# A decoder block on one core: SBUF pools moved by 32 and 96 bytes

## The chip, the core and the metric

The kernel runs on one NeuronCore of a Trainium2 chip. The metric is device time in microseconds for one execution of the whole program. TensorE multiplies, and loads its stationary operand (the weights, `lhsT`) with an instruction of its own that overlaps the matmul before it; the moving operand is the right-hand one (`rhs`). VectorE (DVE), ScalarE (ACT) and GpSimd (POOL) do elementwise work, and SyncE (SP) and ScalarE issue DMAs. All operands of TensorE lie in SBUF, whose 128 partitions each hold a row of bytes; "address" below always means the byte offset within that row, the same in all partitions.

## The reference

One residual block with 2048 positions and a width of 1024, in float32:

```python
mod = silu(c) @ w_mod + b_mod;  shift, scale, gate = split(mod, 3)
h = rms_norm(x, g_norm) * (1 + scale) + shift
x_rnn, z_rnn, q, k, v, z_attn, g_r, g_a = split(h @ w_in, 8)      # each 1024 wide
xc = causal_depthwise_conv(x_rnn)                                   # width 4
y_rnn = (rg_lru(xc) * silu(z_rnn)) @ w_out_rnn                      # gated scan, 8 blocks of 128
o = dilated_attention_mixture(rope(q), rope(k), v)                  # 8 heads of 128, 3 windows
y_attn = (o * silu(z_attn)) @ w_out_attn
merged = sigmoid(g_r + b) * y_rnn + sigmoid(g_a + b) * y_attn
out = rms_norm(x + gate * (merged @ w_o), g_final)
```

## The kernel before, in words

**How a float32 product is made.** Each float32 operand is split into a high part, rounded to the type `float32r`, and a low part that holds the rest. `mm3` (L151 to L154 of the kernel) then makes a product from three matmuls: high by high, high by low, low by high. Every call ends in `mm`, so nearly all matmuls of the profile carry line L149. In a pair of names such as `X<-T,S` the first name is the PSUM tile, and the two behind the arrow are the operands.

**The stages.** The input projection comes first, in two halves `f` of 1024 positions.

- At the start of each half the values `v` are made directly (`values`): the stationary operand is a piece of the normalized activations (tiles `T`, or `b12h` and `b12l`), the moving one is a weight tile `S`, 256 columns wide. A call makes 96 matmuls; there are 16 calls' worth.
- All other columns go through `strassen`, which makes a 2x2 block product with seven multiplications instead of eight. Here the stationary operand is a weight block `S` (seven slots, `S0` to `S6`) and the moving one is an activation block `T` (fourteen slots), 512 columns wide. One multiplication, `prod`, is 12 matmuls in a row: four steps of `mm3`. There are 28 pairs of column blocks, two halves and seven products, so 28 x 2 x 7 x 12 = 4704 matmuls. Between products the rest of the recurrent branch slips in a few: its gates (`xh`, `xl` by `gh`, `gl`), and transposes.
- Then attention, 16 head-halves. It mixes scores (`kq`, `q1`), transposes (`pp` with the identity `cs`) and sums (`pth`, `ptl` by `vh` or `wh`) with the two branch projections, which are fed in a few steps at a time (`steps`): moving `yh` and `yl`, stationary `S`, 512 columns. Two branches, four column blocks each, eight row blocks and 24 matmuls give 1536.
- The end is the output projection (`output`), four quarters of four row blocks, two column halves and eight steps of `mm3`: 768 matmuls, moving `oh` and `ol`, stationary `mh` and `ml`, 512 columns. It alternates with what is left of `steps`, and finishes alone.

**What sets the order.** Inside the input projection and attention the program writes the order out by hand (`manual_schedule`); steps hang on the number of products done (`run_late`, `pump`). Weight blocks are made in the first half (load of `R`, high part on ScalarE at L157, low part on GpSimd at L163, store to DRAM) and loaded again in the second, seven slots ahead (`load_next`). SyncE issues loads and most stores, ScalarE the stores of weight blocks.

**Where tiles lie.** SBUF is filled from both ends. Pools opened on the left stack upward: `cp` (constants), then `hp` with the fourteen slots of `T`, then the working pools of the stage; in attention `ap` and at the end `fp` take the place of `hp`. Pools opened with `side="right"` stack downward: `pS` (`S0` to `S3`), `pR`, `wS` (`S4` to `S6`), `wq`, and later `fl` (`yh`, `yl`). Every tile is rounded up to 32 bytes. The lines that open the pools around the change are L482 to L492:

```python
    B = {}
    hp = pools.open("hp", bufs=1)
    ...
    pS = pools.open("pS", side="right", bufs=1)
    pR = pools.open("pR", side="right", bufs=1)
    wS = pools.open("wS", side="right", bufs=1)
```

The built program gives these first addresses; all other slots of a name follow at multiples of 1024 bytes or more, and the pieces of a tile that one matmul reads start at multiples of 512 bytes in it, so each name has one remainder on division by 256 (only the keys of the window scores start at any multiple of 128 bytes in `kq`):

| operand | role | first address before | modulo 256 | after | modulo 256 |
|---|---|---|---|---|---|
| `T` | moving in `strassen`, stationary in `values` | 18528 | 96 | 18560 | 128 |
| `S0` | stationary in `strassen` and `steps`, moving in `values` | 212960 | 224 | 212864 | 128 |
| `b12h`, first half | stationary in `values` | 149248 | 0 | 149280 | 32 |
| `b12h`, second half | stationary in `values` | 141536 | 224 | 141568 | 0 |
| `yh` | moving in `steps` | 159712 | 224 | 159616 | 128 |
| `oh` | moving in `output` | 18528 | 96 | 18560 | 128 |
| `mh` | stationary in `output` | 108640 | 96 | 108672 | 128 |
| `kq` | both, in scores | 22112 | 96 | 22144 | 128 |
| `pth` | moving in sums | 125856 | 160 | 125888 | 192 |
| `vh` | stationary in sums | 105376 | 160 | 105408 | 192 |
| `xh` | moving in gates | 170144 | 160 | 170176 | 192 |
| `gh` | stationary in gates | 168096 | 160 | 168128 | 192 |

Of the kernel before, what the change touches and what calls it, by code (L numbers as in the profile page):

```python
# [10 lines left out]
F32 = mybir.dt.float32  # L11
# [9 lines left out]
P = 128  # L21
# [68 lines left out]
def decoder_block(ctx, tc, x, c, positions, g_norm, w_mod, b_mod, w_in, b_gate, conv_w, conv_b,  # L90
# [4 lines left out]
    def T(pool, shape, dt, tag, **kw):  # L95
        cnt[0] += 1
        return pool.tile(shape, dt, tag=tag, name=f"{tag}_{cnt[0]}", **kw)
# [25 lines left out]
    cp = ctx.enter_context(tc.tile_pool(name="cp", bufs=1))  # L123
# [32 lines left out]
    def hi_act(o, i):  # L156
        nc.scalar.activation(o, i, AF.Copy)  # L157
# [190 lines left out]
    def strassen(up, f, key, done):  # L348
# [7 lines left out]
        def take():  # L356
            if f:
                return (f, *loaded.pop(0))
            i = next(n_op)
            return f, i, first.pop(i)  # L360

        def prod(ps, b, first, last, op=None):
            f, i, s = op or take()
            bh, bl = B[b]
            for k in range(KH):
# [114 lines left out]


    B = {}  # L482
    hp = pools.open("hp", bufs=1)

    def slot():
        return T(hp, [P, KH, CH], F32R, "T", bufs=14)


    pS = pools.open("pS", side="right", bufs=1)
    pR = pools.open("pR", side="right", bufs=1)  # L490
    wS = pools.open("wS", side="right", bufs=1)
# [35 lines left out]
    def build(st, names, xs, k, first=False, keep=None, pt=None):  # L527

        hh, hl = B[names[k // KH]]
        if pt is None:  # L530
# [13 lines left out]
    def operand(name):  # L544
        B[name] = (slot(), slot())

# [4 lines left out]
    def build_odd(st, xs):  # L551

        B["B12"] = (T(st, [P, KH, CH], F32R, "b12h"), T(st, [P, KH, CH], F32R, "b12l"))
        operand("B22")
        f32 = lambda b, i, k: B[b][i][:, k, :].bitcast(F32)
        tt = nc.vector.tensor_tensor
# [8 lines left out]
        def split(name, k, t):  # L565
            hh, hl = B[name]
            hi_act(hh[:, k, :], t)
            lo_dve(hl[:, k, :], t, hh[:, k, :])
# [1326 lines left out]
```

## Time and profile before

| | |
|---|---|
| median of three runs | 2258.73 us |
| lowest, highest | 2254.85, 2258.97 us |
| span of the profiled execution | 2256.2 us |
| the profiled execution's own time | not given beside its span; the span lies between the lowest and the highest run |
| TensorE busy | 2212.2 us, 98% of the span, 11422 matmuls |
| weight loads busy | 1856.8 us, 82% |
| VectorE, ScalarE, GpSimd busy | 1346.9 (60%), 1257.3 (56%), 977.8 us (43%) |
| mean granted TensorE clock | 0.992 |

A matmul's duration in the profile is longer than its share of the time, because each starts while the one before it drains: a 512-column matmul is shown with some 395 ns, but the next starts some 230 ns after it did. So the number to read is the distance from start to start. The view in order of time merges equal instructions in a row into one line with the first one's start, the time to the last one's end and their count; the difference of two lines' starts, divided by the matmuls between, gives that distance.

### The profile page before, as it was taken

How to read it: one execution, taken by the hardware profiler on the slowest of the kernel's cores; microseconds unless marked ns; L12 is line 12 of the kernel's file. 1: busy time of each engine (PE TensorE's matmuls, PEld its weight loads, DVE VectorE, ACT ScalarE, POOL GpSimd, SP SyncE). 2: the span in 40 equal slices, each digit the busy share in tenths (PEclk: the TensorE clock that was granted, in tenths of full speed). 3: DMA queues.
4: the chain of work that ended last, by engine and by line, in shares of the span. 5: the costliest groups of instructions: out<-in, count | busy, mean ns of one | idle time of the engine just before them, and what ended most of it. 6: DMA issues, size and time to landing. Idle time of an engine off the chain costs nothing.

```text
span 2256.2 us, 33998 instructions
## 1 busy us (share of the span) xinstructions
PE 2212.2 (98%) x11422; PEld 1856.8 (82%) x11422; DVE 1346.9 (60%) x2380; ACT 1257.3 (56%) x2481; POOL 977.8 (43%) x734
## 2 busy tenths in 40 slices
PE   8999999999999999999999999999999998999998
PEld 5988888888878988888888877888889887978887
DVE  5838877778555815444445343566667877666443
ACT  6638668668543627556546302677778887533211
POOL 2457676767557422222223102455566655332100
PEclk9999999999999999999999999999999999999999
DMA  8367887887998378888888988988888897899442
GB/s 286 115 219 255 281 290 260 291 277 262 326 277 292 110 235 267 278 279 272 283 280 278 332 291 277 287 252 256 263 269 262 241 264 217 255 329 285 153 132 89
DMA packets 428626, 573.64 MB, mean 254 GB/s; under 512 B 72134, under 2 KB 292514, under 8 KB 427428
## 3 DMA queue, kind: packets, MB, share of 16 engines
q1 hardware_dynamic: 390612, 451.73, 64.9%
q10 hardware_dynamic: 37648, 119.70, 13.8%
q8 instruction: 90, 1.47, 0.3%
q14 instruction: 84, 0.69, 0.1%
q0 software_dynamic: 192, 0.05, 0.0%
HBM read 357.44 MB, written 213.91 MB: 253 GB/s over the span
## 4 chain that ended last, share of the span: by engine, by line
PE 58%; DMA 4%; DVE 2%; issue 2%; ACT 2%; POOL 2%; SPq 1%; ACTq 0%; POOLq 0%; DVEq 0%
PE pj L149 11%; PE X L149 9%; PE V L149 8%; PE pq L149 8%; PE Z L149 4%; PE W L149 4%; PE sc L149 4%; PE Y L149 4%; PE o L149 4%; DMA vraw<-vN 1%; PE pT L1498 1%; PE pg L149 1%; DMA meT<-fg 1%; PE pT L1511 1%; DMA kraw<-qT 1%
## 5 line engine op out<-in xcount | busy, mean ns | idle before, releaser
L149 PE MATMUL pj<-yh,S 128*128 128x512 f32 x1024 | 370.0, 405 | 10.5 <-ACT yh L157 4.6
L149 PE MATMUL V<-T,S 128*128 128x512 f32 x1344 | 330.8, 395 | 1.7 <-DVE t L450 1.7
L149 PE MATMUL X<-T,S 128*128 128x512 f32 x1344 | 331.3, 395 | 0.9 <-POOL S L163 0.9
L163 POOL TENSOR_TENSOR S<-R,S 128x512 fp32r<-128x512 f32 x168 | 253.5, 1516 | 171.6 <-ACT S L157 70.3
L149 PEld LDWEIGHTS V<-T,S 128*128 128x128 f32 x1344 | 252.6, 188 | 61.9 <-DVE t L450 2.3
L149 PEld LDWEIGHTS X<-T,S 128*128 128x128 f32 x1344 | 252.4, 188 | 61.2 <-POOL S L163 1.7
L149 PEld LDWEIGHTS pj<-yh,S 128*128 128x128 f32 x1024 | 194.3, 190 | 49.4 <-ACT yh L157 6.1
L149 PE MATMUL pj<-yl,S 128*128 128x512 f32 x512 | 202.9, 396 | 6.1 <-POOL yl L163 5.1
L1414 ACT ACTIVATE pp<-pp,st 128x256 f32<-128x256 f32 (+3 forms) x256 | 133.8, 524 | 95.8 <-DVE st L1413 94.8
L163 POOL TENSOR_TENSOR S<-s,S 128x512 fp32r<-128x512 f32 x84 | 128.6, 1531 | 121.7 <-ACT S L157 77.8
L149 PE MATMUL Z<-T,S 128*128 128x512 f32 x672 | 165.8, 395 | 0.0
L149 PE MATMUL Y<-T,S 128*128 128x512 f32 x672 | 165.7, 395 | 0.0
L149 PE MATMUL W<-T,S 128*128 128x512 f32 x672 | 165.4, 395 | 0.0
L149 PEld LDWEIGHTS W<-T,S 128*128 128x128 f32 x672 | 126.3, 188 | 30.1 <-issue 0.9
L149 PEld LDWEIGHTS Z<-T,S 128*128 128x128 f32 x672 | 126.3, 188 | 29.4
L149 PEld LDWEIGHTS Y<-T,S 128*128 128x128 f32 x672 | 126.4, 188 | 29.2
L166 DVE TENSOR_TENSOR ptl<-pT,pth 128x384 fp32r<-128x384 f32 (+1 forms) x160 | 97.9, 628 | 75.6 <-ACT pth L157 73.4
L163 POOL TENSOR_TENSOR s<-R,s 128x512 fp32r<-128x512 f32 x32 | 46.5, 1452 | 204.9 <-ACT s L157 201.8
L157 ACT ACTIVATE S<-R 128x512 fp32r<-128x512 f32 x168 | 101.8, 622 | 47.4 <-DMA R<-in_w_in_dram 21.6
L905 DVE SCALAR_TENSOR_TENSOR xc<-xr,par,xc 128x512 f32<-128x512 f32 x96 | 95.6, 996 | 47.3 <-ACT xc L899 45.0
L1478 ACT ACTIVATE pp<-pp,M 128x256 f32<-128x256 f32 (+3 forms) x256 | 117.9, 522 | 10.0 <-DVE M L1601 10.0
L1413 DVE CUSTOM_DVE_ANT_0 pp<-sc,msk 128x256 f32<-128x256 f32 (+3 forms) x256 | 104.7, 449 | 24.6 <-PE sc L149 22.1
(334 smaller groups left out, 4729.9 us busy)
## 6 DMA issues: line engine op xcount, KB each, us to landing
sD<-S ACTq DMA_DIRECT2D x196, 512.0 KB, 4.1
S<-sD SPq DMA_DIRECT2D x196, 512.0 KB, 4.9
S<-wD SPq DMA_DIRECT2D x100, 512.0 KB, 5.7
R<-in_w_in_dram SPq DMA_DIRECT2D x136, 256.0 KB, 4.3
wD<-s ACTq DMA_DIRECT2D x64, 256.0 KB, 5.1
T<-in_w_mod_dram SPq DMA_DIRECT2D x8, 1024.0 KB, 12.0
vN<-ev SPq DMA_DIRECT2D x64, 128.0 KB, 2.8
zaT<-ev SPq DMA_DIRECT2D x32, 256.0 KB, 4.1
```

The source lines that it names most:

```text
L149: nc.tensor.matmul(o, lhsT=l, rhs=r, start=st, stop=sp, **kw)
L157: nc.scalar.activation(o, i, AF.Copy)
L163: nc.gpsimd.tensor_tensor(o, i, h.bitcast(F32), ALU.subtract)
L166: return nc.vector.tensor_tensor(o, i, h.bitcast(F32), ALU.subtract).ins
L905: nc.vector.scalar_tensor_tensor(xc, xr[:, i : i + CH], cw(i), xc, ALU.mult, ALU.add)
L1413: nc.vector.tensor_tensor_reduce(pdst, s_ps, mask, 1.0, 3e38, ALU.add, ALU.min, m_)
L1414: nc.scalar.activation(pdst, pdst, AF.Exp, bias=m_, scale=-1.0, accum_out=l_)
L1478: nc.scalar.activation(pp, pp, AF.Copy, scale=w)
L1498: nc.tensor.transpose(pt[:, c0 + j * P : c0 + (j + 1) * P], pp[i][:, k * P : (k + 1) * P], ident)
L1511: nc.tensor.transpose(pt[:, c * P : (c + 1) * P], pp[:, half * P : (half + 1) * P], ident)
```

## The change: two unused tiles that move everything behind them

A tile of 8 floats (32 bytes) is added at the end of the constants' pool, ahead of `hp`, and a new pool with a tile of 24 floats (96 bytes) ahead of all pools on the right. Nothing writes or reads either tile. The instructions of every engine, their order and their waits are the same as before; only addresses differ. What is opened on the left behind `cp` starts 32 bytes later, and everything on the right 96 bytes earlier. The constants themselves (`cs`, `par`, `ones`) stay where they were.

```diff
     B = {}
+    T(cp, [P, 8], F32, "shift")
     hp = pools.open("hp", bufs=1)
...
+    shift = ctx.enter_context(tc.tile_pool(name="shift", bufs=1, side="right"))
+    T(shift, [P, 24], F32, "shift")
     pS = pools.open("pS", side="right", bufs=1)
```

## The prediction

> **What bounds the kernel now.** I read the page's busy times first, then its slices, then the waits of TensorE, then the view in order of time, which gives what the others hide: the distance from one matmul's start to the next one's.
>
> ```profile
> span 2256.2 us, 33998 instructions
> PE 2212.2 (98%) x11422; PEld 1856.8 (82%) x11422; DVE 1346.9 (60%) x2380; ACT 1257.3 (56%) x2481; POOL 977.8 (43%) x734
> ...
> DVE  5838877778555815444445343566667877666443
> ACT  6638668668543627556546302677778887533211
> POOL 2457676767557422222223102455566655332100
> PEclk9999999999999999999999999999999999999999
> ```
>
> TensorE is busy 98% of the span, and its clock is granted in full. No other engine reaches nine tenths in a slice. In the stage of the products (`strassen`, roughly 140 to 700 us and 820 to 1380 us) TensorE waits for almost nothing:
>
> ```profile
> engine line waited for: us in total, times, longest us
> PE V L149 <- DVE t L450: 1.7, 3, 1.2
> PE X L149 <- POOL S L163: 0.9, 1, 0.9
> ```
>
> These are all its waits between 140 and 700 us; between 830 and 1340 us the same view has none. So what counts there is how densely matmuls follow each other. First the products, stationary `S` at 224 modulo 256 and moving `T` at 96; then, in the same view, a stretch of the branch projection, stationary `S` at 224 and moving `yh` and `yl` at 224 too:
>
> ```profile
> 1215.47 2.94 PE L149 MATMUL V<-T,S 128*128 128x512 f32 x12
> ...
> 1232.20 2.02 PE L149 MATMUL W<-T,S 128*128 128x512 f32 x8
> ```
>
> ```profile
> 1390.17 0.61 PE L149 MATMUL pj<-yh,S 128*128 128x512 f32 x2
> ...
> 1397.65 0.61 PE L149 MATMUL pj<-yh,S 128*128 128x512 f32 x2
> ```
>
> Between the first pair of lines lie six products of 12: 16.73 us / 72 = 232.4 ns a matmul. Between the second lie eleven steps of three: 7.48 us / 33 = 226.7 ns. Same type, same 512 columns, the same `S` tiles, and DMA is busy in both. The output projection, both operands at 96, agrees with the second; the chain of waits gives its last stretch, and a piece of the branch projection before it:
>
> ```profile
> 2155.38 5.45 PE pj L149 x24
> 2160.83 87.06 PE pq L149 x384
> ```
>
> 87.06 us / 384 = 226.7 ns, and 5.45 / 24 = 227.1 ns. So operands that are equal modulo 256 run at 226.7 ns whether their residue is 96 or 224, and the pair that differs by 128 runs at 232.4 ns. After a disturbance the products even stay in a worse rhythm:
>
> ```profile
> 1361.38 2.96 PE L149 MATMUL Y<-T,S 128*128 128x512 f32 x12
> 1364.18 2.96 PE L149 MATMUL X<-T,S 128*128 128x512 f32 x12
> 1366.98 2.26 PE L149 MATMUL V<-T,S 128*128 128x512 f32 x9
> ```
>
> That is 5.60 us / 24 = 233.3 ns. The values, 256 columns wide, show the relation too: the stationary tile `b12h` of the second half is at 224 like the moving `S`, the tiles `T` are at 96.
>
> ```profile
> 770.77 2.88 PE V L149 x24
> ```
>
> ```profile
> 773.48 3.01 PE L149 MATMUL X<-S,T 128*128 128x256 f32 x24
> 776.33 3.01 PE L149 MATMUL V<-S,T 128*128 128x256 f32 x24
> ```
>
> Equal residues take 2.88 / 24 = 120.0 ns, unequal ones (776.33 - 773.48) / 24 = 118.8 ns: here equality costs 1.2 ns. These two lines also say which modulus matters. Modulo 512, `b12h` is at 224 and `S` at 480; they differ by 256 and still have the rhythm of their own. After the change `T` and `S` stand the same way, at 128 and 384 modulo 512.
>
> **The products.** The change removes no instruction, adds none and moves none past another; the order on all five queues is the old one. What it alters is addresses. `S` and `T` are both at 128 modulo 256 afterwards. I take the 226.7 ns of the branch projection, the nearest row: the same stationary tiles, the same width, the same three-matmul steps. 4704 matmuls x (232.4 - 226.7) ns = 26.8 us less, all on the path, since TensorE waits for nothing there. The bounds are nothing gained (0) and the 233.3 ns of the disturbed rhythm, left everywhere (30.9 us).
>
> **Regaining the rhythm.** Gates and transposes interrupt the products some 50 times (32 groups of gate matmuls and about 20 of transposes). Even with equal residues the first matmuls after an interruption are slower:
>
> ```profile
> 1387.88 0.40 PE L149 MATMUL pj<-yl,S 128*128 128x512 f32 x1
> ```
>
> This is the second matmul after a pause; from it to the line at 1390.17 above, ten matmuls take 2.29 us, 23 ns more than ten at 226.7 ns. I take 20 ns for each interruption, 1.0 us in all, between 0 and twice that.
>
> **The values.** 1152 of the 1536 matmuls have a stationary `T`, and these become equal: 1152 x 1.2 ns = 1.4 us more. `b12h` and `b12l` in the second half lose their equality (192 matmuls, 0.2 us less); in the first half they go from 0 to 32 against a moving tile that goes from 224 to 128, between the two rows shown, so within 0.2 us. Together +1.2 us, between 0 and 2.
>
> **Attention and output.** The pairs in scores, sums, gates, branch projection and output are equal modulo 256 before and after. What changes for them is the remainder modulo 64, from 32 to 0, and no row shows two operands at multiples of 64. I cost that at nothing. Its lower end is the densest rhythm that the trace has at 512 columns, the warm-up matmuls in bf16:
>
> ```profile
> 7.41 1.68 PE L149 MATMUL V<-busy 128*128 128x512 bf16 x7
> ```
>
> With the last one's 0.38 us taken off, six distances in 1.30 us are 217 ns, 9.7 ns under 226.7. If alignment gave all of that, the products, the branch projections and the output (4704 + 1536 + 768 = 7008 matmuls) would save 68 us more. Nothing excludes a loss of the same size either. I take zero because the equal pairs at 96 and at 224 do not differ: beyond equality no remainder shows in the trace, though both of these are 32 modulo 64 and so cannot speak for 0.
>
> **Engines and queues.** TensorE asking 2.5% earlier needs the others to follow. The tightest 100 us:
>
> ```profile
> 200.00:300.00 100.00, 100.00 (x432) 81.08 (x432) 87.54 (x99) 73.54 (x117) 73.73 (x49) 1.00 0.82 277
> 1200.00:1300.00 100.00, 100.00 (x432) 81.11 (x431) 46.64 (x63) 46.80 (x69) 22.46 (x17) 1.00 0.93 307
> ```
>
> DVE goes from 87.5 to about 90 of 100, ScalarE and GpSimd to about 75.5, the DMA share from 0.93 to 0.95. The loads of `S` in the second half are what a shorter product would expose first:
>
> ```profile
> S<-sD SPq DMA_DIRECT2D x196, 512.0 KB, 4.9
> ```
>
> A load lands 4.9 us after its issue, and seven slots give it six products, 6 x 12 x 226.7 ns = 16.3 us. Were that cover gone, each late load would cost up to 4.9 - 2.7 us. I cost it at nothing.
>
> **The sum.** -26.8 + 1.0 + 1.2 = -24.6 us. Against the span that is 2231.6. The span is 2.5 us under the median of 2258.73 and inside the three runs, so I carry the difference over: 2234 us.
>
> **What the Trainium skill says to this.** "TensorE: Matmul & The Clock Gate", section "Step-by-step: what each phase is for", says that the engine has two independent read ports, one for the streaming operand and one for weight loads, so that loading the next weights takes no bandwidth from the running matmul. By that rule addresses would not matter and the time would stay at 2258.7. The trace disagrees: 232.4 against 226.7 ns for the same instruction. "SBUF — State Buffer", section "Specifications (TRN2)", gives cachelines of 16 bytes. By that, operands at 32 and at 0 modulo 64 both start on a line, and alignment would neither save the 68 us nor cost them; no run here shows it.
>
> **The rivals.**
>
> *Alignment helps as well.* The 226.7 ns is itself above the 217 ns of the bf16 row, and something fills that gap; a start in the middle of a 64-byte unit could be part of it. For it: operands at 32 modulo 64 are all the trace has. Against it: `b12h` in the first half is at a multiple of 64, and its rhythm is no outlier. 24 matmuls took 2.84 us there (118.3 ns):
>
> ```profile
> 93.26 0.40 PE L149 MATMUL W<-S,b12h 128*128 128x256 f32 x2
> ...
> 96.10 0.40 PE L149 MATMUL X<-S,b12h 128*128 128x256 f32 x2
> ```
>
> In full it gives 2166 us, by half 2200 us.
>
> *Slower.* Weights and moving operand start at the same place of a unit, at its very beginning, and each weight read holds the stream up for longer. The place is every matmul whose operands are equal. If what is above 217 ns doubled, all 7008 would run at 236.4 ns: the products 4.0 ns x 4704 = 18.8 us more, the other 2304 9.7 ns more, 22.3 us; 2258.7 + 41 = 2300 us. It decides from about 3.5 ns a matmul (24.6 us / 7008). For it: the equal 256-column pairs are slower by 1.2 ns. Against it: the equal 512-column pairs are faster, at both residues.
>
> *Nothing happens.* What differs between products and branch projection is then not the remainder but something else of these tiles, such as how far apart they lie, or a modulus of 512. Against it: `b12h` and `T` share the same loop and the same moving tile, and still differ. It gives 2259 us.
>
> **How the numbers follow.** Chances: the sum as it stands 0.71, alignment helping too 0.14, nothing 0.06, slower 0.09. The likeliest is 2234 us; its own range, with 0 to 2 us for each small term and the chance that not all products reach 226.7 ns, is 2228 to 2244. The range for 8 in 10 takes in half of the second case and all of "nothing": 2200 to 2260. A measurement of this kernel can tell about 0.2%, 4.5 us, from no change. So faster 0.85, within it 0.06, slower 0.09.
>
> **What would show it.** In the changed kernel a product of 12 should take 2.72 us from start to start instead of 2.79; the values with `T` 120.0 ns instead of 118.8; the last 384 matmuls of the output again 87.1 us. If those 87.1 us move, alignment matters, and each of the 7008 matmuls has moved with them; that, above 3.5 ns either way, is what would put the prediction far off. If the product stays at 2.79 us, the residue was not the cause. Waits of TensorE on `S` or on DVE in the products would mean that the cover was thinner than I read it.

## The result, and the profile after

The changed kernel is faster. Its median is 2238.38 us against 2258.15 us of the kernel before on the same chip; the ratio is 0.9914 with a 95% interval of 0.9893 to 0.9935. A second measurement, with five rounds, gave 2241.36 against 2260.53 us and 0.9916 (0.9902 to 0.9929). The prediction was 2234 us, with 2228 to 2244 for its likeliest case: right in sign and cause, and the gain of 24.6 us was about 5 us too large.

The profiled execution took 2235.07 us, its span is 2233.3 us. The page's first lines after the change:

```profile
span 2233.3 us, 33998 instructions
PE 2185.9 (98%) x11422; PEld 1851.1 (83%) x11422; DVE 1348.6 (60%) x2380; ACT 1256.2 (56%) x2481; POOL 978.3 (44%) x734
```

TensorE is still the bound, at 98%, and its busy time is 26.3 us shorter. In order of time, products in the second half behind a group of gate matmuls (first start in us, time to the end of the last, line, names, count):

```profile
1200.44 2.91 PE L149 MATMUL V<-T,S 128*128 128x512 f32 x12
1203.18 2.88 PE L149 MATMUL X<-T,S 128*128 128x512 f32 x12
...
1216.79 2.88 PE L149 MATMUL W<-T,S 128*128 128x512 f32 x12
```

From 1203.18 to 1216.79 lie five products: 13.61 us / 60 = 226.8 ns a matmul, where the kernel before had 232.4. The first product after the gates takes 2.74 us to the next start instead of 2.72, so regaining the rhythm costs 20 ns. The values with `T`, and the last stretch of the output in the chain of waits:

```profile
767.04 3.04 PE L149 MATMUL X<-S,T 128*128 128x256 f32 x24
769.92 3.04 PE L149 MATMUL V<-S,T 128*128 128x256 f32 x24
```

```profile
2132.52 5.44 PE pj L149 x24
2137.96 87.05 PE pq L149 x384
```

The values take 2.88 us / 24 = 120.0 ns, as forecast. The output takes 87.05 us instead of 87.06: its operands moved from 96 to 128 modulo 256, from 32 to 0 modulo 64, and nothing came of it.

What was not forecast are these waits of TensorE between 140 and 700 us:

```profile
PE V L149 <- DVE t L450: 3.5, 3, 1.9
PE X L149 <- POOL S L163: 1.9, 2, 1.0
PE X L149 <- ACT u L383: 0.7, 2, 0.5
PE V L149 <- DVE ev L450: 0.2, 1, 0.2
```

Together they are 6.3 us, where the kernel before had 2.6. All of them lie between 570 and 690 us, near the end of the first half. The view by stages shows what else is true there (window, then busy time of TensorE, weight loads, DVE, ScalarE and GpSimd, granted clock, DMA share, GB/s), first before and then after:

```profile
560.00:600.00 40.00, 40.00 (x173) 32.42 (x173) 22.52 (x26) 23.51 (x38) 23.96 (x17) 1.00 0.92 305
600.00:640.00 40.00, 38.60 (x164) 30.32 (x163) 26.63 (x40) 21.33 (x37) 24.03 (x16) 1.00 0.95 315
```

```profile
560.00:600.00 40.00, 39.09 (x170) 31.40 (x169) 18.36 (x25) 21.93 (x34) 20.85 (x15) 1.00 1.00 321
600.00:640.00 40.00, 36.79 (x160) 29.37 (x159) 24.63 (x37) 22.23 (x38) 26.48 (x18) 1.00 0.93 308
```

The DMA engines are nearly full, at 0.92 to 1.00 before and after, and the elementwise engines are not: DVE is busy 18 to 27 of 40 us. When the starts of the same matmul in the two traces are set side by side, the first half's products gain 8.9 us up to 542 us on the clock of before, lose 1.2 us in the rest of that half, and the second half gains 12.2 us.

That the waits are longer than in the trace of before cannot be put down to the change alone, because this stretch differs much from one execution to the next. A second trace of the change (`e8_again`) has 6.6 us of waits there, but the kernel "Aligned, but 128 apart" of the next section, whose products keep the old rhythm, has 5.0 us too:

```profile
PE X L149 <- POOL S L163: 3.6, 1, 3.6
PE X L149 <- ACT u L383: 1.1, 1, 1.1
PE V L149 <- DVE t L450: 0.3, 1, 0.3
```

Against the trace of before, that kernel loses 4.9 us in the rest of the first half, and the second trace of the change 3.0 us. What the traces do show is that the denser products, worth 8.9 us up to 542 us in both traces of the change, gained nothing in that rest. The remaining difference of single traces is not to be read: the start of the program and attention differ by up to 4 us from one execution to the next.

### The profile page after: what moved, and what is told of

It reads as the page before. It is cut to its first block, busy times and chain, and to the rows that moved or that the text cites. A ratio compares the mean times of both kernels' runs of the same rounds, so it can differ in the third digit from the quotient of the medians.

```text
span 2233.3 us, 33998 instructions
## 1 busy us (share of the span) xinstructions
PE 2185.9 (98%) x11422; PEld 1851.1 (83%) x11422; DVE 1348.6 (60%) x2380; ACT 1256.2 (56%) x2481; POOL 978.3 (44%) x734
## 4 chain that ended last, share of the span: by engine, by line
PE 55%; DMA 6%; DVE 3%; ACT 3%; issue 2%; POOL 2%; SPq 1%; ACTq 0%; POOLq 0%; DVEq 0%
PE pj L149 11%; PE X L149 8%; PE V L149 7%; PE pq L149 7%; PE sc L149 4%; PE W L149 4%; PE Z L149 4%; PE o L149 4%; PE Y L149 3%; PE pT L1501 1%; DMA R<-in_w_in_dram 1%; PE pg L149 1%; PE pT L1514 1%; POOL S L163 1%; DMA gaT<-ev 1%
## 5 line engine op out<-in xcount | busy, mean ns | idle before, releaser
L149 PE MATMUL V<-T,S 128*128 128x512 f32 x1344 | 324.6, 390 | 3.7 <-DVE t L450 3.5
L149 PE MATMUL X<-T,S 128*128 128x512 f32 x1344 | 324.5, 390 | 2.9 <-POOL S L163 1.9
```

The lines of the kernel that those rows point to most:

```text
L149: nc.tensor.matmul(o, lhsT=l, rhs=r, start=st, stop=sp, **kw)
```

## Is it equality, or alignment?

The change does two things to the products' operands: it makes them equal modulo 256, and it puts them at multiples of 64. Two kernels do one of these alone, and a third kernel measures the relation by itself.

**Equal, but at 32 modulo 64.** The tile on the left is left out, the one on the right has 32 floats.

```diff
-    T(cp, [P, 8], F32, "shift")
...
-    T(shift, [P, 24], F32, "shift")
+    T(shift, [P, 32], F32, "shift")
```

> No tile on the left, one of 32 floats on the right: T and S both at 96 modulo 256, equal as in the change, but 32 off a multiple of 64. Theory (equality alone): the products run at 226.7 ns, a product of 12 in 2.72 us, and the time is that of the change, 2238 us within 5. Rival (alignment to 64 carries part of it): the products stay above 228 ns and the time lies between 2243 and 2258 us.

Measured: 2238.70 us, ratio 0.9917 (0.9899 to 0.9935), the same as the change. In order of time, two lines of its products:

```profile
1003.04 2.88 PE L149 MATMUL X<-T,S 128*128 128x512 f32 x12
1005.76 2.88 PE L149 MATMUL Y<-T,S 128*128 128x512 f32 x12
```

A product takes 2.72 us. Multiples of 64 are not needed.

**Aligned, but 128 apart.** The column of ones goes into a spare column of the constants, which takes 32 bytes off the left, and the tile on the right has 8 floats.

```diff
-    cs = T(cp, [P, N_CST_A], F32, "cs")
+    cs = T(cp, [P, N_CST_A + 1], F32, "cs")
...
-    ones = T(cp, [P, 1], F32, "ones")
+    ones = cs[:, N_CST_A : N_CST_A + 1]
...
-    T(cp, [P, 8], F32, "shift")
...
-    T(shift, [P, 24], F32, "shift")
+    T(shift, [P, 8], F32, "shift")
```

> The column of ones is moved into the constants' tile, which takes 32 bytes off the left, and a tile of 8 floats goes in on the right: T at 64 and S at 192 modulo 256, every operand at a multiple of 64, and the two 128 apart as before the change. Theory (equality alone): the products run at 232.4 ns and the time is that of the kernel before, 2258 us within 5. Rival (alignment alone): 226.7 ns and 2238 us.

Measured: 2258.53 us, ratio 1.0008 (0.9998 to 1.0017), the time of the kernel before.

```profile
1000.75 2.95 PE L149 MATMUL V<-T,S 128*128 128x512 f32 x12
1003.54 2.96 PE L149 MATMUL Z<-T,S 128*128 128x512 f32 x12
1006.33 2.94 PE L149 MATMUL W<-T,S 128*128 128x512 f32 x12
```

A product takes 2.79 us again. Alignment to 64 alone does nothing; equality alone gives the whole measured gain.

**The relation by itself.** A kernel with nothing but matmuls, each stretch 72 of them in the pattern of `mm3`, with the start of both operands chosen.

```python
for s in range(STEPS):
    for k in range(KH):
        for j, (l, r) in enumerate(((0, 0), (0, 1), (1, 0))):
            lo = b + (l * KH + k) * P        # b: place of the weights
            ro = a + (r * KH + k) * CH       # a: place of the moving operand
            nc.tensor.matmul(ps[:, :n], lhsT=weights[:, lo : lo + P], rhs=moving[:, ro : ro + n], ...)
```

> This kernel leaves the whole block out: it copies x to the output and runs stretches of 72 matmuls of the products' three-matmul pattern, with two operands placed at chosen addresses, no other engine at work. Theory (equality modulo 256 sets the rhythm): a stretch whose two operands are equal modulo 256 runs at 226.7 ns a matmul, whatever the common residue (0, 32, 48, 96), and also when they differ by 256 modulo 512; the difference of 128 runs at 232 to 233 ns. At 256 columns equality gives 120.0 ns and 128 apart 118.6 ns. Rival (alignment to 64 counts as well): with equal operands, residue 0 is at least 2 ns apart from residue 32. Rival (the independent ports of the Trainium skill, page TensorE: Matmul & The Clock Gate, section Step-by-step: what each phase is for): all 512-column stretches are alike within 1 ns.

Measured, in order of time; from the line at 32.72 on, the weights start 0, 32, 64, ... 256 bytes behind the moving operand modulo 512:

```profile
32.72 16.49 PE L65 MATMUL b<-moving,weights 128*128 128x512 f32 x72
49.05 16.95 PE L65 MATMUL a<-moving,weights 128*128 128x512 f32 x72
65.84 16.96 PE L65 MATMUL b<-moving,weights 128*128 128x512 f32 x72
82.64 17.02 PE L65 MATMUL a<-moving,weights 128*128 128x512 f32 x72
99.50 16.89 PE L65 MATMUL b<-moving,weights 128*128 128x512 f32 x72
116.23 16.96 PE L65 MATMUL a<-moving,weights 128*128 128x512 f32 x72
133.03 16.66 PE L65 MATMUL b<-moving,weights 128*128 128x512 f32 x72
149.53 16.96 PE L65 MATMUL a<-moving,weights 128*128 128x512 f32 x72
166.32 16.49 PE L65 MATMUL b<-moving,weights 128*128 128x512 f32 x72
182.65 16.95 PE L65 MATMUL a<-moving,weights 128*128 128x512 f32 x72
```

The first stretch of all, from 13.42 us on, is left out: it has the same pair as the second and took 19.30 us, 268.1 ns a matmul; why it is slow stays open. The difference of two starts, divided by 72, with the other stretches worked out the same way:

| weights behind moving, modulo 256 | 0 | 32 | 64 | 96 | 128 | 160 | 192 | 224 |
|---|---|---|---|---|---|---|---|---|
| 512 columns, ns | 226.8 | 233.2 | 233.3 | 234.2 | 232.4 | 233.3 | 229.2 | 233.2 |
| 256 columns, ns | 119.9 | 118.3 | 117.8 | 117.4 | 118.8 | 120.0 | 117.8 | |

Behind 256 the row repeats (226.8 at 256), and with the moving operand at 32 instead of 0 it is the same within 0.3 ns. Equality at 96 gives 227.4 with the first few matmuls counted in. So the relation is the difference modulo 256, at any common place that is a multiple of 32. Off these multiples it breaks: both operands at 16 give 230.0 ns, at 48 233.2, at 8 231.9, at 4 237.9. No other engine works beside these stretches. The transfers of the copy are over after 93 us (the DMA share is 0.00 from 100 to 200 us), and the row from 166 us on, without them, repeats the one begun at 32.72 us within 0.1 ns. The numbers are those of the kernel, so neither DMA nor another engine has a part in it.

## Where the rest of the gain went

**Fewer stores near the end of the first half.** The theory: the DMA engines are full there, so what feeds the products arrives late, and the products cannot be faster than it. The blocks of the last 7 of 28 pairs are not stored, in the changed kernel and in the kernel before.

```diff
+    KEPT = 21 * 7
...
-                nc.scalar.dma_start(sD[k], t2[:].bitcast(F32))
+                if k < KEPT:
+                    nc.scalar.dma_start(sD[k], t2[:].bitcast(F32))
-            while 7 * x + i == 28 * 7 - 1 and kept:
-                k, t2 = kept.pop(0)
-                nc.scalar.dma_start(sD[k], t2[:].bitcast(F32))
...
-            nc.sync.dma_start(t[:].bitcast(F32), sD[n])
+            nc.sync.dma_start(t[:].bitcast(F32), sD[n % KEPT])
```

> The changed kernel, with the stores of the weight blocks of the last 7 of 28 pairs left out (49 stores of 512 KB); the second half loads other blocks in their place, as many and as large, so a part of its products is computed from wrong weights. Theory (the gain of the products is given back near the end of the first half because the DMA engines are full there): TensorE's waits between 545 and 700 us fall from 8 us to under 3, and the time falls by 4 to 7 us below the changed kernel's 2238. Rival (VectorE, ScalarE and GpSimd are at their limit there, whatever DMA does): the waits stay above 5 us, and the time stays within 2 us of 2238.

> The same stores left out in the kernel before the change, with wrong weights in the same products. Theory (full DMA engines): its waits there were 3.4 us on the products and go too, so it falls to some 2254, and stands 24 to 26 us above the changed kernel with the same stores left out, the whole of the predicted gain. Rival (other engines): the distance stays at 20 us.

Measured: 2228.87 us and 2253.15 us, 24.3 us apart. The changed kernel gains about 9.5 us from the missing stores, more than expected, and the kernel before gains 5.4. TensorE's waits between 545 and 700 us and two stages, of the changed kernel with fewer stores:

```profile
PE X L149 <- ACT u L382: 0.3, 1, 0.3
PE V L149 <- DVE ev L449: 0.3, 1, 0.3
```

```profile
560.00:600.00 40.00, 39.43 (x173) 32.03 (x172) 21.97 (x29) 24.14 (x38) 22.36 (x16) 1.00 0.74 209
600.00:640.00 40.00, 40.00 (x178) 33.16 (x177) 29.91 (x41) 23.84 (x40) 30.65 (x21) 1.00 0.52 107
```

The waits fall from 6.3 to 0.6 us although DVE, ScalarE and GpSimd do more in 600 to 640 us than in the change with all its stores. In the kernel before they fall to none. Set side by side, the two traces without the stores differ by 8.9 us up to 542 us, by 2.6 us in the rest of the first half and by 12.9 us in the second half. So the stores hold that stretch, not the elementwise engines, and without them the change is worth 24.3 us. A store that is left out takes its bytes from the DMA engines, and it also gives its slot back sooner; which of the two counts stays open.

**The load of x, ten products later.** Which of the transfers could make way? The load of `x` moves by ten products (`DELAY = 10`), its norm by 10 or 11.

```diff
-        xs = load_x(xp, 2, "x", 2)
+        xs = []
+        for r in range(0, 4, 2):
+            t = T(xp, [P, 2, D], F32, "x", bufs=2)
+            later(DELAY + r, lambda t=t, r=r: nc.sync.dma_start(t[:], xv[2, r : r + 2].rearrange("r j d -> j r d")))
+            xs += [t[:, 0, :], t[:, 1, :]]
...
-            later(5 + r, lambda r=r: square(r))
+            later(DELAY + 6 + r, lambda r=r: square(r))
```

> The changed kernel, with the 2 MB of x for the third quarter loaded 10 products later, where the DMA engines have less else to do, and its norm worked out 6 to 8 products later. Nothing is left out. Theory (full DMA engines): the first waits of that stretch, 2.7 us between 574 and 615 us, become shorter and the time falls by 1 to 4 us. Rival: the waits move with the load, and the time stays within 1 us of the changed kernel.

Measured: 2242.86 us, ratio to the kernel before 0.9931 (0.9918 to 0.9945), where the change has 0.9914 and 0.9916. So it is not faster; that it is slower is not shown, as the intervals overlap. TensorE's waits between 545 and 700 us:

```profile
PE X L149 <- ACT u L384: 9.2, 4, 4.2
PE V L149 <- DVE ev L451: 0.2, 1, 0.2
```

The waits did not just move with the load: they are 9.4 us, against 6.3 and 6.6 in the two traces of the change. They now nearly all stand behind ScalarE's copies of `X` (`u`). The longest:

```profile
639.07 5.25 PE L149 MATMUL X<-T,S 128*128 128x512 f32 x12 [4.21 <-ACT u L384]
```

The copy comes right behind the issue of a weight block's store, which waits in ScalarE's queue, and ScalarE is idle ahead of it:

```profile
638.04 0.33 ACTq L276 DMA_DIRECT2D sD<-S  x1
638.41 0.60 ACT L384 ACTIVATE u<-X 128x512 f32<-128x512 f32 x1 [2.08 <-DMA qT<-t]
```

At the next long wait the picture is the same: store at 663.30 us, copy at 663.68 us, ScalarE idle for 4.01 us. The squares of `x` ran from 634.1 to 650.2 us, so ScalarE's work on them is not what held that copy. What held the stores is not shown. The granted clock fell to 0.91 between 640 and 680 us, and the product behind the wait took 5.25 us to its end where others take 2.88, so a wait costs more than its own length here. Neither theory had this.

**Five products ahead instead of four.**

```diff
-    LEAD = 4
+    LEAD = 5
```

> The changed kernel with one number altered: weight blocks are loaded and split five products ahead of their use instead of four. Nothing is left out. Theory (near the end of the first half full DMA engines make blocks late): one more product of 2.7 us as cover takes away part of the 8 us of waits there, and the time falls by 2 to 5 us below the changed kernel. Rival (the seven slots are all taken, so an earlier start only blocks GpSimd and ScalarE sooner): the waits stay or grow, and the time is the same within 2 us or longer.

> The changed kernel itself, beside the next run on the same chip. Both theories: 2238 us within 4, 20 us under the kernel before.

Measured: 2253.04 us against 2241.36 us for the change itself. The rival was right: it is longer, by 11.7 us. The waits between 140 and 735 us:

```profile
PE X L149 <- ACT u L383: 7.7, 6, 3.9
PE V L149 <- DVE t L450: 2.1, 2, 1.4
PE V L149 <- DVE ev L450: 1.5, 2, 0.8
PE pg L1021 <- DVE ev L1016: 1.1, 1, 1.1
PE pg L527 <- DVE hf L544: 0.9, 1, 0.9
PE pg L149 <- POOL xl L163: 0.5, 1, 0.5
```

Some of them lie at 256 and 396 to 426 us, where the change has none at all. At the first of them, ScalarE's copy of `X` at 255.30 us ran right behind a split at 254.78 us, with no pause before either, so splits do stand ahead of a copy there; that this is behind all the waits is not shown. Nor do the waits alone make up the 11.7 us: they are 13.8 us, where `e8_again` has 8.2 in the same window. The product behind the wait of 1.84 us at 256 us took 4.61 us to its end instead of 2.88. Neither attempt beats the change.

## What makes the rhythm

The theory here: the next weights are read while the moving operand streams, and the two get in each other's way. Then fewer columns of weights should cost less, and the pair that counts should be a moving operand with the weights of the next matmul.

> The block is left out again: x is copied, and stretches of 72 matmuls run at 512 columns with 128, 96, 64 or 32 columns of weights, and in bf16 with 128. Theory (what is left above 217 ns, and what the residues change, is the weight load's reading beside the stream's): with equal residues the distance falls in step with the weights, from 226.7 ns at 128 columns to about 222 at 64 and 219 at 32; the 128-apart distance falls from 232.4 towards the same; in bf16, which reads half the bytes, all differences give 216 to 217 ns. Rival (a fixed cost of a matmul of this type): 226.7 ns at every width of the weights.

The edit, beside the map above, is the slice of the weights (`lhsT=wt[:, lo : lo + cols]`), and tiles in bf16. Measured from start to start, in ns:

| columns of weights | 128 | 96 | 64 | 32 |
|---|---|---|---|---|
| equal | 226.7 | 230.1 | 230.0 | 231.4 |
| 128 apart | 232.5 | 231.7 | 229.4 | 230.7 |

The theory's numbers failed: with fewer columns the distance does not fall towards 217, and the special place of equality is gone. The rival's constant 226.7 failed too. In bf16 all differences are alike:

```profile
168.26 15.71 PE L73 MATMUL b_-128_735<-short,light 128*128 128x512 bf16 x72
183.81 15.70 PE L73 MATMUL a_-128_808<-short,light 128*128 128x512 bf16 x72
199.35 15.70 PE L73 MATMUL b_-128_881<-short,light 128*128 128x512 bf16 x72
```

That is 15.55 and 15.54 us / 72, or 216.0 and 215.8 ns, equal and 64 apart; 128 apart begins with the third line.

> The block is left out: x is copied, and stretches of 72 matmuls at 512 columns take turns between two places of the operands. Theory (what counts is the stream beside the load of the next weights, so the moving operand of one matmul against the stationary one of the next): turns in which each matmul's own pair differs by 128 but its moving operand equals the next weights run at 226.7 ns; turns in which each matmul's own pair is equal but the next weights differ by 128 run above 229 ns; the same for 64. Rival (a matmul's own pair counts): the two swap.

The edit lets the places `a` and `b` take turns with each matmul. The two stretches with turns of 128, and the start of the next:

```profile
64.76 16.61 PE L66 MATMUL b<-moving,weights 128*128 128x512 f32 x72
81.20 16.72 PE L66 MATMUL a<-moving,weights 128*128 128x512 f32 x72
97.76 16.86 PE L66 MATMUL b<-moving,weights 128*128 128x512 f32 x72
```

Measured: own pair equal and the next weights 128 off, 228.3 ns; own pair 128 off and the next weights equal, 230.0 ns; for 64, 231.8 and 233.3 ns. Neither is 226.7, and the turns in which the own pair is equal are the faster ones. The theory that only the next weights count falls, and so does the plain rival. Two more stretches let only one operand take turns between 0 and 128: 232.2 ns with the weights, 230.0 ns with the moving operand. In both, half of the matmuls have an equal own pair and half have equal next weights, so one price for each of these two would have made them alike. In these runs 226.7 to 227.4 ns was seen at 512 columns and full width of weights only where all operands of a stretch were in line.

So it is shown that the difference modulo 256 sets the distance of float32r matmuls of 512 columns with 128 columns of weights, at places that are multiples of 32, and that bf16 does not care at the three differences measured. What in the reading of the operands makes it so stays open, as does why equal float32r matmuls take 10.9 ns more than bf16 ones.

## Why the prediction was right, point by point

- **What bounds the kernel**: right. TensorE's density in the products, not a wait, was what the change could move.
- **The products, 26.8 us**: the mechanism and the size per matmul were right, 226.8 ns against the 226.7 taken from the branch projection. What failed is that all 4704 matmuls would turn it into time. (The upper bound of 30.9 us is 31.0 by its own 233.3 and 226.7 ns; nothing hangs on it.)
- **Engines and queues, costed at nothing**: this is the step that failed. The prediction read its tightest stages at 200 to 300 and 1200 to 1300 us and found every cover sufficient. The stage that mattered was 560 to 680 us, where the DMA share before was already 0.92 to 0.96 and TensorE already waited 2.6 us; there the change left waits of 6.3 us, and denser products gained nothing. The measured gain is 19.8 us, and 24.3 us without the stores of that stretch, so about 4.5 us were not earned; by the interval of the second measurement it is some 2 to 8 us. The sum of 24.6 us was the gain with the cover in place. The prediction did name the sign, waits on `S` or DVE in the products, and put a late load at up to 2.2 us, but it costed the whole at nothing. That 2238 us still lies in its own range is owed to an allowance for products that do not all reach 226.7 ns, not to this stretch having been foreseen.
- **Regaining the rhythm, 20 ns each**: right where it was read, 2.74 us against 2.72 for a product behind the gates.
- **The values, 1.2 us more**: right for a matmul, 120.0 ns as in the row of `b12h`.
- **Attention and output, nothing**: right for alignment. 87.05 against 87.06 us, and both kernels that part alignment from equality say the same.
- **The rivals**: "alignment helps as well" and "slower" fall with the two kernels and the map. "Nothing happens", with its modulus of 512, falls too: 256 apart is as good as equal.
- **Ports and cachelines**: the Trainium skill, "TensorE: Matmul & The Clock Gate", section "Step-by-step: what each phase is for", has two independent read ports, and a weight load that takes nothing from the running matmul. If addresses then do not matter, as the prediction drew from it, the runs agree in bf16 (216.0 and 215.8 ns) and not in float32r (226.8 to 234.2 ns by place). The Trainium skill, "SBUF — State Buffer", section "Specifications (TRN2)", has cachelines of 16 bytes. By these alone all multiples of 16 would be alike; with equal operands the runs have 226.8 ns at 0 and 227.1 at 32, but 230.0 at 16 and 233.2 at 48.

## What to carry to other kernels

Where a kernel is bound by float32r matmuls of 512 columns, look at the distance from start to start in each stage and at the addresses of both operands: weights and moving operand equal modulo 256, at multiples of 32, gave 2.4% in the stage that had them 128 apart, for two unused tiles. At 256 columns equality was the slowest place but one, 2% behind the best (119.9 against 117.4 ns), so it is worth measuring per shape. And when the bounding engine gets denser, read the stage in which its feeders are fullest, not a typical one: here about a quarter of the first half kept back about a fifth of the gain.

## What the runs showed of the hardware that was not expected

- The rhythm of float32r matmuls depends on the operands' addresses at all: 226.8 ns when equal modulo 256, 229.2 at 192, 232.4 to 234.2 at other multiples of 32, and up to 237.9 ns when both are 4 bytes off.
- An equal pair finds its rhythm by itself: after another pair, stretches of 72 took 16.33, 16.35 and 16.37 us (differences 256, then both at 32, both at 96), at most 40 ns more than the 16.33 us of one that followed an equal pair. The pair 128 apart has more than one rhythm: 232.4 ns, and 233.3 ns in the products of before after a disturbance.
- A wait can cost more than its length: the products behind waits of 1.84 us (`e9_lead_five`) and 4.21 us (`e6_later_x`) took 4.61 and 5.25 us to their end instead of 2.88. Behind one of 1.92 us in the change it was 2.99, so the length of the wait alone does not decide it.
- Narrower weights were not faster: 230.0 ns at 64 columns against 226.7 at 128, with equal operands.
